# A two-layer hybrid trunk on one core: the high part of the modulated activations moves to ScalarE, the masked B to another pool, the zero states to DRAM

## The chip, the cores and the metric

One core of a Trainium2 chip runs the whole program in one launch. The metric is the device time of one execution in microseconds; the kernel before takes 3178.77 us (median of three runs).

## What is computed

The reference is a trunk of two layers over 1024 latent tokens and 256 context tokens of width 1024, in float32. Cut to what matters here:

```python
for l in range(DEPTH):
    u_ctx = modulate(rmsnorm(h_ctx, norm_mix_pre[l]), m_ctx[0], m_ctx[1])
    u_lat = modulate(rmsnorm(h_lat, norm_mix_pre[l]), m_lat[0], m_lat[1])
    a_ctx, a_lat = mixer_block(u_ctx, u_lat, ...)
    h_lat = h_lat + m_lat[2] * rmsnorm(a_lat, norm_mix_post[l])
    v_lat = modulate(rmsnorm(h_lat, norm_ffn_pre[l]), m_lat[3], m_lat[4])
    f_lat = conv_ffn(v_lat, ...)
    h_lat = h_lat + m_lat[5] * rmsnorm(f_lat, norm_ffn_post[l])
    ...
```

`mixer_block` projects u with one matrix into three groups of heads, a bidirectional Mamba-2 SSD, a neighbourhood attention and a bidirectional HGRN2, and joins their outputs in one output projection. In the second layer the context is not carried further. The SSD works in chunks of 128 tokens: for a chunk

```python
scores = jnp.einsum('btgn,bsgn->btsg', c_c, b_c)
y = jnp.einsum('btsg,btsgh,bsghp->btghp', scores, decay, x_c)
y = y + jnp.einsum('btgn,bghnp->btghp', c_c, h) * jnp.exp(cum)[..., None]
```

where h is the state that enters the chunk; it is zero for the first chunk of each direction.

## The kernel before

Tokens are cut into three blocks: block 0 is the context (two tiles of 128 tokens), blocks 1 and 2 hold four tiles of latent tokens each. Matrix products are made in three terms, since the fast operand type (fp32r) keeps only the leading bits of a float32: each activation and each weight is split into a high part H, rounded to fp32r, and a low part L, the float32 value less H; the products are H·wH, L·wH and H·wL.

**Modulated activations.** `xn_to_u` (L498) turns normalized token tiles into the transposed, modulated activations u. For each of eight tiles of 128 features TensorE transposes into a PSUM tile of tag "m"; ScalarE reads it, applies scale and shift and writes x into the SBUF tile S_xu (L168); `split(..., "p")` (L485) has GpSimd copy x, rounded, into U_uH (L490), and VectorE writes U_uL = x - H (L177). In some calls x is also stored to uD. The calls are made at the start, in the post that ends each mixer (layer 0 and layer 1), where u feeds the FFN, and in the post before layer 1: 136 feature tiles in all, of which 16, at the start, have 512 columns and 120 have 256. `post` (L539) runs around these calls: squares for the norm on ScalarE (the tile "junk", L168, with a short read of the accumulator), residual additions on GpSimd (L589), scaling of normalized tiles on GpSimd (L496) and ScalarE. "A unit" below is one call with two token tiles, eight feature tiles of 256 columns.

**The SSD outputs.** The scan over chunks leaves the entering states in a D tile, D_Us, and stores them to DRAM (hsD). Then `ssd_body` (L1365) goes through the chunks with a lag of three (SSD_LAG). For a chunk `ssd_load` (L1290) takes a D tile "sc" of five slices: slice 0 the two entering states, loaded from hsD or, for the first chunk of a direction, cleared by GpSimd (L1297); slice 1 the inputs (xtD); slices 2 and 3 hold ei, written by `ssd_weights`; half of slice 4 the two masked copies of B, made by GpSimd in `pmask` (L1287), one for each group g. `ssd_weights` (L1312) makes the weights of a group: S_R with D_sv and with the constant scr give exponents in "m" tiles (the matmuls S_R,D_sv and scr), ScalarE takes their exponential into S_E, GpSimd adds both directions (L1332), the matmul pg (L1330; F_cv,D_sc in the rows) multiplies the masked B by C, and VectorE multiplies. `ssd_outputs` then multiplies with states and inputs (S_E,D_sc and D_sc in the rows, L1342 on). The output projection's first half, `out_first` (L1458), is woven into this body as its filler (`weave`, L84): its products F_wo,U_m and w_wo,U_m stand between the SSD's own on TensorE. Its weights come through `load_wo` (L1429): four `wr` tiles for each half, loaded from DRAM and split into H and L. `mix_second` (L1410) takes `wr` tiles named gate.

**What sets the order.** All SBUF tiles come from one pool by tag, with a fixed number of buffers, and a tile waits until the buffer's last reader is done. All loads and stores are issued by SyncE (L163) in one queue. The order on each engine is fixed when the program is built, by the framework's timeline simulation (`schedule_with_timeline_sim=True`, L1930); on the chip every engine runs its own list in order and waits at its head. The numbers of buffers:

```python
BUFS = {"U": 10, "F": 10, "D": 3, "wr": 4, "w": 4, "S": 8, "E": 3, "O": 1}
PB = {"g": 2, "m": 6}
```

Of the kernel before, what the change touches and what calls it, by code (L numbers as in the profile page):

```python
# [8 lines left out]
F32 = mybir.dt.float32  # L9
# [4 lines left out]
AF = mybir.ActivationFunctionType  # L14
ALU = mybir.AluOpType
# [113 lines left out]
class Kern:  # L129
# [368 lines left out]
    def xn_to_u(self, b, xns, mod, u=None, o0=0, keep=None):  # L498

        n = 128 * len(xns)  # L500
        who = 1 if b == 0 else 0
        u = u or self.new_u(b)
        for ft in range(KT):
            pp = self.p("m")
            for i, xn in enumerate(xns):
                o = 128 * (ft % 4)
                self.tr(pp[:, 128 * i:128 * i + 128], xn[ft // 4][:, o:o + 128])
            x = self.t("S", [128, 512], name="xu")[:, 0:n]
            self.act(x, pp[:, 0:n], AF.Identity, scale=mod[:, who, 1, ft:ft + 1], bias=mod[:, who, 0, ft:ft + 1])
            self.split(u["H"][ft][:, o0:o0 + n], u["L"][ft][:, o0:o0 + n], x, "p")  # L510
            if keep is not None and b:
                self.dma(keep[ft, :, BLK[b][0] + o0:BLK[b][0] + o0 + n], x)
        return u
# [775 lines left out]

    def ssd_load(self, c, rows, cols, B):  # L1290
        tsl = slice(128 * c, 128 * c + 128)
        u = self.t("D", [128, 5, 512], name="sc")
        xz = self.t("F", [128, 2, 4, 128], name="xz")
        for d, i in ((0, c), (1, ORD_B.index(c))):
            hp = slice(64 * d, 64 * d + 64)
            if i == 0:
                self.nc.gpsimd.memset(u[hp, 0, :], 0.0)  # L1297
            else:
                self.dma(u[hp, 0, :], self.hsD[i, hp, :])
        self.dma(u[:, 1, :], self.xtD[tsl, :])  # L1300
        self.dma(xz[:, 0], self.xD[:, :, tsl].rearrange("j p t -> p j t"))
        self.dma(xz[:, 1], self.zD[:, :, tsl].rearrange("j p t -> p j t"))
        r = self.t("S", [128, 4, 128], F32R, name="R")
        self.pmask(r, rows[:, tsl].bitcast(F32), self.scs[:, 0:4], 4)
        o = 512 * (c % 2)
        cs = cols[:, 1, o:o + 512].rearrange("p (a b) -> p a b", b=128)
        self.pmask(cs, cols[:, 0, tsl].bitcast(F32), self.scs[:, 4:8], 4)
        o = 128 * c + (1 if c < 2 else 2)
        self.pmask(u[:, 4, 0:256].rearrange("p (a b) -> p a b", b=128), B[:, o:o + 128], self.scs[:, 8:10], 2)
        return u, xz, r, cs  # L1310

    def ssd_weights(self, Cm, c, g, u, r, cs):  # L1312

        o0 = 128 * c + (1 if c < 2 else 2)
        csl = slice(o0, o0 + 128)
        Es = []
        for d in range(2):
            ps = self.p("m")
            self.mm(ps, cs[:, 2 * g + d, :], r, stop=False)
            self.mm(ps, self.identr, self.late[d].unsqueeze(1).to_broadcast([128, 4, 128]), start=False)  # L1320
            e = self.t("S", [128, 4, 128], name="E")
            self.act(e.rearrange("p a b -> p (a b)"), ps, AF.Exp)
            Es.append(e)
        ps = self.p("m")
        self.mm(ps, self.sel[g], r)
        ei = u[:, 2 + g, :]
        self.act(ei, ps, AF.Exp)
        ei = ei.rearrange("p (h t) -> p h t", h=4)
        pg = self.p("m")
        self.mm(pg[:, 0:128], u[:, 4, 128 * g:128 * g + 128], Cm[g][:, csl])  # L1330
        w = Es[0]
        self.nc.gpsimd.tensor_tensor(out=w, in0=w, in1=Es[1], op=ALU.add)  # L1332
        self.nc.vector.tensor_tensor(out=ei, in0=ei, in1=Cm[g][:, csl].unsqueeze(1).to_broadcast([128, 4, 128]), op=ALU.mult)
        self.tt(w, w, pg[:, 0:128].unsqueeze(1).to_broadcast([128, 4, 128]), ALU.mult)
        return w, ei
# [461 lines left out]
    def run(self):  # L1797
        A = self.A
        self.adaD, self.adaP, self.adaN, self.ada_pend, self.ada_todo = {}, {}, {}, [], []
        self.consts()  # L1800
        self.cond()
        X, Wh = [], []
        mod = self.first_mod({2: lambda: X.append(self.first_norm(0)),
                              KT - 1: lambda: Wh.append(self.load_wt(0, *HEAD[0]))})
        Wh.append(self.load_wt(0, *HEAD[1]))
        self.more_consts()
        X.append(self.first_norm(1))
        U = {0: self.xn_to_u(0, X[0], mod)}
        X.append(self.first_norm(2))
        for b in (1, 2):  # L1810
            U[b] = self.xn_to_u(b, X[b], mod)
        C = {0: self.layer_cols(0)}
        self.lower_bounds()
        h1 = [self.dram([T, DM], f"h1_{l}") for l in range(2)]
        h2 = self.dram([T, DM], "h2")
        self.mixD = self.dram([8, 128, T], "mixD")
        self.zD = self.dram([4, 128, T], "zD")
        self.xD = self.dram([4, 128, T], "xD")
        self.accD = self.dram([T, DM], "accD")
        self.uD = self.dram([KT, 128, T], "uD")  # L1820
        self.hidD = [self.dram([NT, 128, len(grp), 128], f"hid{p}") for p, grp in enumerate(PASSES)]
        self.gD = self.dram([2, 128, T], "gD")
        self.iD = self.dram([T, 256], "iD")
        self.xtD = self.dram([T, 512], "xtD")
        self.vD = self.dram([T, 256], "vD")
        self.cvD = self.dram([2, 32, T], "cvD")
        self.hsD = self.dram([NT, 128, 512], "hsD")
        self.ada_todo = [(0, i, kt, q) for i in (1, 2) for q in range(4) for kt in range(KT)]
        for l in range(2):
            clo = 0 if l == 0 else 2  # L1830
            lat = [0, 1, 2] if l == 0 else [1, 2]
            U = self.layer(l, U, C, clo, lat, h1, h2, Wh)
# [102 lines left out]
```

## Time and profile before

| what | value |
|---|---|
| time, median of three runs | 3178.77 us (3176.94 to 3183.29) |
| time of the profiled execution | 3183.62 us |
| span of the profiled execution | 3181.8 us |
| mean clock granted to TensorE, of full speed | 0.973 |
| TensorE matmuls busy | 3013.4 us, 95% |
| VectorE busy | 1851.6 us, 58% |
| ScalarE busy | 1347.9 us, 42% |
| GpSimd busy | 769.8 us, 24% |

The profile is of one execution; its span begins with the first and ends with the last instruction, and the time is 1.8 us longer. Busy shares are means over stages that have different limits. In the rows PE is TensorE, PEld its weight loads, DVE is VectorE, ACT ScalarE, POOL GpSimd and SP SyncE; an entry in brackets at the end of a timeline row is the time the engine was idle before it and what ended that. Names are those of the program's tiles, tag first: U_uH is the high part of u.

### The profile page before, as it was taken

Reading aid. Unit: us, or ns where it says so; the run is one execution under the profiler, and the core shown is the slowest. Engines: PE = TensorE matmul, PEld = TensorE weight load, DVE = VectorE, ACT = ScalarE, POOL = GpSimd, SP = SyncE. Lnnn points to the kernel's source line nnn. Section 1 sums busy time; section 2 is a strip of 40 time slices with the busy share of each in tenths; the row PEclk is TensorE's granted clock in tenths of the full one; section 3 lists DMA queues with packets and bytes.
Section 4 is the critical chain, followed back from the end, with each engine's and each line's share of the span. In section 5 each row is a group of like instructions: output and inputs, shape, how many; then the busy total and the mean of one; then the engine's idle time right before and its main releaser. Section 6 shows DMA issues by size and latency. Waiting matters only on the chain. (4 is left out here: it accounts for less than half of the span.)

```text
span 3181.8 us, 55600 instructions
## 1 busy us (share of the span) xinstructions
PE 3013.4 (95%) x21478; PEld 2468.8 (78%) x21478; DVE 1851.6 (58%) x3443; ACT 1347.9 (42%) x2605; POOL 769.8 (24%) x847
## 2 busy tenths in 40 slices
PE   6999999979999999998999899999989899999998
PEld 4977877767778888886777797777767788887886
DVE  5253544568876665563344826554668876667346
ACT  4225625644543333343112633745545544445222
POOL 2000101146423333330000400101254344442002
PEclk8999999989999999999999999999999999999999
DMA  6224143366552222236465412221457532224242
GB/s 239 85 87 112 44 120 92 118 187 195 190 180 65 65 75 70 68 89 183 147 184 166 128 46 79 58 77 55 123 181 225 170 93 82 82 80 142 85 134 96
DMA packets 440649, 373.59 MB, mean 117 GB/s; under 512 B 28188, under 2 KB 360880, under 8 KB 439360
## 3 DMA queue, kind: packets, MB, share of 16 engines
q1 hardware_dynamic: 440384, 370.04, 38.4%
q8 instruction: 169, 2.77, 0.4%
q14 instruction: 96, 0.79, 0.1%
HBM read 265.17 MB, written 95.30 MB: 113 GB/s over the span
## 5 line engine op out<-in xcount | busy, mean ns | idle before, releaser
L189 PE MATMUL m_p<-U_dw,S_hH 128*128 128x512 f32 x1296 | 405.6, 392 | 1.2 <-ACT S_hH L171 1.2
L189 PE MATMUL g_p<-U_uH,w_wH 128*128 128x512 f32 (+1 forms) x1192 | 288.3, 375 | 26.3 <-POOL U_uH L490 13.5
L189 PE MATMUL m_p<-U_uH,w_wo 128*128 128x512 f32 x1120 | 306.5, 396 | 0.0
L189 PEld LDWEIGHTS m_p<-U_dw,S_hH 128*128 128x128 f32 x1296 | 243.6, 189 | 56.1 <-issue 3.8
L189 PE MATMUL g_p<-U_uL,w_wH 128*128 128x512 f32 (+1 forms) x1192 | 274.0, 367 | 0.0
L189 PE MATMUL g_p<-U_uH,w_wL 128*128 128x512 f32 (+1 forms) x1192 | 269.9, 362 | 2.0 <-issue 2.0
L189 PEld LDWEIGHTS g_p<-U_uH,w_wH 128*128 128x128 f32 x1192 | 206.5, 197 | 71.1 <-POOL U_uH L490 20.3
L189 PE MATMUL m_p<-U_dw,S_hL 128*128 128x512 f32 x648 | 254.2, 392 | 1.4 <-DVE S_hL L177 1.4
L189 PEld LDWEIGHTS m_p<-U_uH,w_wo 128*128 128x128 f32 x1120 | 207.9, 188 | 47.4 <-issue 0.2
L189 PEld LDWEIGHTS g_p<-U_uL,w_wH 128*128 128x128 f32 x1192 | 204.6, 198 | 34.3 <-issue 2.3
L189 PEld LDWEIGHTS g_p<-U_uH,w_wL 128*128 128x128 f32 x1192 | 199.9, 192 | 37.3 <-issue 4.2
L189 PE MATMUL m_p<-D_su,w_wo 128*128 128x512 f32 x800 | 206.2, 395 | 0.0
L177 DVE TENSOR_TENSOR w_wo<-wr_wr,w_wo 128x512 fp32r<-128x512 f32 x168 | 144.4, 860 | 102.4 <-ACT w_wo L171 101.7
L186 DVE SCALAR_TENSOR_TENSOR F_fc<-F_raw,colB,F_fc 128x1281 f32<-128x1281 f32 (+3 forms) x102 | 162.2, 1591 | 51.6 <-ACT F_fc L168 51.4
L177 DVE TENSOR_TENSOR S_hL<-S_hL,S_hH 128x512 fp32r<-128x512 f32 (+1 forms) x90 | 69.4, 771 | 189.6 <-ACT S_hH L171 189.4
L171 ACT CAST S_hH<-S_hL 128x512 fp32r<-128x512 f32 (+1 forms) x90 | 59.7, 663 | 278.7 <-DMA S_hL<-hid 254.9
L189 PEld LDWEIGHTS m_p<-D_su,w_wo 128*128 128x128 f32 x800 | 148.9, 188 | 34.1
L171 ACT CAST w_wo<-wr_wr 128x512 fp32r<-128x512 f32 x168 | 103.3, 619 | 160.3 <-PE m_p L189 101.1
L189 PE MATMUL m_p<-F_su,w_wo 128*128 128x512 f32 x640 | 161.7, 394 | 0.0
L1642 POOL TENSOR_TENSOR wr_t<-E_wr,E_wr 128x512 f32<-128x512 f32 x40 | 56.3, 1408 | 403.7 <-DMA E_wr<-in_ffn_w_up 335.5
L189 PE MATMUL m_p<-U_uL,w_wo 128*128 128x512 f32 x560 | 153.5, 395 | 0.0
L189 PEld LDWEIGHTS m_p<-U_dw,S_hL 128*128 128x128 f32 x648 | 122.0, 188 | 29.3 <-issue 2.2
(377 smaller groups left out, 6217.1 us busy)
## 6 DMA issues: line engine op xcount, KB each, us to landing
wr_aw<-in_ada_w SPq DMA_DIRECT2D x160, 256.0 KB
wr_wr<-in_ffn_w_up SPq DMA_DIRECT2D x96, 256.0 KB
wr_wr<-in_w_in SPq DMA_DIRECT2D x88, 256.0 KB
wr_wrd<-in_ffn_w_down SPq DMA_DIRECT2D x88, 256.0 KB
E_wr<-in_ffn_w_up SPq DMA_DIRECT2D x80, 256.0 KB
hid<-S_u SPq DMA_DIRECT2D x80, 256.0 KB
S_hL<-hid SPq DMA_DIRECT2D x54, 256.0 KB
h<-D_acc SPq DMA_DIRECT2D x45, 256.0 KB
```

What stands on the lines that cost most here:

```text
L171: self.nc.scalar.copy(out, in_)
L177: self.nc.vector.tensor_tensor(out=out, in0=a, in1=b, op=op)
L186: self.nc.vector.scalar_tensor_tensor(out=out, in0=a, scalar=s, in1=b, op0=op0, op1=op1)
L189: self.nc.tensor.matmul(out, lhsT=lhsT, rhs=rhs, start=start, stop=stop)
L1642: padd = lambda o, x, y, op=ALU.add: gp.tensor_tensor(out=o, in0=x, in1=y, op=op)
```

## The change

It has three parts. In `xn_to_u` ScalarE reads the PSUM tile twice, once into U_uH with rounding and once into S_xu; GpSimd's copy at L490 goes, VectorE's subtraction stays. The PSUM tile is held until the second read. In `ssd_load` the D tile has four slices, and the masked B goes to a tile mb of tag "wr", 128 x 256, held until the second group's pg matmul (a D buffer keeps its size, which other tiles of the tag set). The zero states are loaded like the others: a tile of zeros is written to hsD[0] at the start, and the two clears by GpSimd become two loads of 128 KB.

```diff
--- before.py
+++ after.py
@@ -506,8 +506,10 @@
                 o = 128 * (ft % 4)
                 self.tr(pp[:, 128 * i:128 * i + 128], xn[ft // 4][:, o:o + 128])
             x = self.t("S", [128, 512], name="xu")[:, 0:n]
-            self.act(x, pp[:, 0:n], AF.Identity, scale=mod[:, who, 1, ft:ft + 1], bias=mod[:, who, 0, ft:ft + 1])
-            self.split(u["H"][ft][:, o0:o0 + n], u["L"][ft][:, o0:o0 + n], x, "p")
+            h = u["H"][ft][:, o0:o0 + n]
+            for y in (h, x):
+                self.act(y, pp[:, 0:n], AF.Identity, scale=mod[:, who, 1, ft:ft + 1], bias=mod[:, who, 0, ft:ft + 1])
+            self.tt(u["L"][ft][:, o0:o0 + n], x, h.bitcast(F32), ALU.subtract)
             if keep is not None and b:
                 self.dma(keep[ft, :, BLK[b][0] + o0:BLK[b][0] + o0 + n], x)
         return u
@@ -1289,14 +1291,11 @@
 
     def ssd_load(self, c, rows, cols, B):
         tsl = slice(128 * c, 128 * c + 128)
-        u = self.t("D", [128, 5, 512], name="sc")
+        u = self.t("D", [128, 4, 512], name="sc")
         xz = self.t("F", [128, 2, 4, 128], name="xz")
         for d, i in ((0, c), (1, ORD_B.index(c))):
             hp = slice(64 * d, 64 * d + 64)
-            if i == 0:
-                self.nc.gpsimd.memset(u[hp, 0, :], 0.0)
-            else:
-                self.dma(u[hp, 0, :], self.hsD[i, hp, :])
+            self.dma(u[hp, 0, :], self.hsD[i, hp, :])
         self.dma(u[:, 1, :], self.xtD[tsl, :])
         self.dma(xz[:, 0], self.xD[:, :, tsl].rearrange("j p t -> p j t"))
         self.dma(xz[:, 1], self.zD[:, :, tsl].rearrange("j p t -> p j t"))
@@ -1306,10 +1305,11 @@
         cs = cols[:, 1, o:o + 512].rearrange("p (a b) -> p a b", b=128)
         self.pmask(cs, cols[:, 0, tsl].bitcast(F32), self.scs[:, 4:8], 4)
         o = 128 * c + (1 if c < 2 else 2)
-        self.pmask(u[:, 4, 0:256].rearrange("p (a b) -> p a b", b=128), B[:, o:o + 128], self.scs[:, 8:10], 2)
-        return u, xz, r, cs
-
-    def ssd_weights(self, Cm, c, g, u, r, cs):
+        mb = self.t("wr", [128, 256], name="mb")
+        self.pmask(mb.rearrange("p (a b) -> p a b", b=128), B[:, o:o + 128], self.scs[:, 8:10], 2)
+        return u, xz, r, cs, mb
+
+    def ssd_weights(self, Cm, c, g, u, r, cs, mb):
 
         o0 = 128 * c + (1 if c < 2 else 2)
         csl = slice(o0, o0 + 128)
@@ -1327,7 +1327,7 @@
         self.act(ei, ps, AF.Exp)
         ei = ei.rearrange("p (h t) -> p h t", h=4)
         pg = self.p("m")
-        self.mm(pg[:, 0:128], u[:, 4, 128 * g:128 * g + 128], Cm[g][:, csl])
+        self.mm(pg[:, 0:128], mb[:, 128 * g:128 * g + 128], Cm[g][:, csl])
         w = Es[0]
         self.nc.gpsimd.tensor_tensor(out=w, in0=w, in1=Es[1], op=ALU.add)
         self.nc.vector.tensor_tensor(out=ei, in0=ei, in1=Cm[g][:, csl].unsqueeze(1).to_broadcast([128, 4, 128]), op=ALU.mult)
@@ -1825,6 +1825,9 @@
         self.vD = self.dram([T, 256], "vD")
         self.cvD = self.dram([2, 32, T], "cvD")
         self.hsD = self.dram([NT, 128, 512], "hsD")
+        zero = self.t("S", [128, 512], name="zero")
+        self.nc.gpsimd.memset(zero, 0.0)
+        self.dma(self.hsD[0], zero)
         self.ada_todo = [(0, i, kt, q) for i in (1, 2) for q in range(4) for kt in range(KT)]
         for l in range(2):
             clo = 0 if l == 0 else 2
```

Line numbers after the change are larger by two or three (L1287 becomes L1289). The order on the engines moves with it. Three places are shown, before and after, each as one piece of the list of one engine.

GpSimd, layer 0, as the SSD outputs begin (D_sc is the chunk's tile, F_cv holds B, wr_gate belongs to `mix_second`, E_xw to the scan; S_R is the first chunk's mask of the row sums). Before:

```order
L1252 TENSOR_TENSOR E_xw_7266<-S_xT_7194,tdt_1581 128x512
L1297 MEMSET D_sc_7606 64x512
L1252 TENSOR_TENSOR E_xw_7281<-S_xT_7260,tdt_1581 128x512
L1287 TENSOR_TENSOR D_sc_7606<-F_cv_6033,scs_263 128x256
L1424 TENSOR_TENSOR wr_gate_7468<-U_m_7460,wr_gate_7468 128x512
L1424 TENSOR_TENSOR wr_gate_7474<-U_m_7460,wr_gate_7474 128x512
L1252 TENSOR_TENSOR E_xw_7449<-S_xT_7346,tdt_1581 128x256
L1252 TENSOR_TENSOR E_xw_7522<-S_xT_7429,tdt_1581 128x512
L1287 TENSOR_TENSOR S_R_7613<-F_sr_6590,scs_263 128x512
```

After:

```order
L1254 TENSOR_TENSOR E_xw_7269<-S_xT_7197,tdt_1584 128x512
L1289 TENSOR_TENSOR wr_mb_7619<-F_cv_6036,scs_263 128x256
L1254 TENSOR_TENSOR E_xw_7284<-S_xT_7263,tdt_1584 128x512
L1289 TENSOR_TENSOR wr_mb_7667<-F_cv_6036,scs_263 128x256
L1424 TENSOR_TENSOR wr_gate_7471<-U_m_7463,wr_gate_7471 128x512
L1424 TENSOR_TENSOR wr_gate_7477<-U_m_7463,wr_gate_7477 128x512
L1289 TENSOR_TENSOR wr_mb_7740<-F_cv_6036,scs_263 128x256
L1289 TENSOR_TENSOR wr_mb_7849<-F_cv_6036,scs_263 128x256
L1254 TENSOR_TENSOR E_xw_7452<-S_xT_7349,tdt_1584 128x256
L1254 TENSOR_TENSOR E_xw_7525<-S_xT_7432,tdt_1584 128x512
L1289 TENSOR_TENSOR S_R_7616<-F_sr_6593,scs_263 128x512
```

The clear is gone, and the masks of four chunks, in the four `wr` buffers, stand ahead of the first chunk's S_R; before, one mask did.

SyncE, the same place (wr_wr<-in_w_out are weights of `out_first`, second half; accD<-E_o stores its results; hsD<-D_Us stores the states). Before, the four weights are issued long ahead of the states' store:

```order
L164 DMA xtD_615<-S_xT_7260 128x4x128
L164 DMA wr_wr_7914<-in_w_out 128x512
L164 DMA wr_wr_7918<-in_w_out 128x512
L164 DMA accD_606<-E_o_7408 128x512
L164 DMA wr_wr_7924<-in_w_out 128x512
L164 DMA wr_wr_7928<-in_w_out 128x512
L164 DMA accD_606<-E_o_7432 128x512
```

After, they stand behind that store and between the loads of the chunks:

```order
L164 DMA hsD_618<-D_Us_7143 64x9x256 x2
L164 DMA wr_wr_7921<-in_w_out 128x512
L164 DMA accD_606<-E_o_7810 128x512
L164 DMA D_sc_7609<-hsD_618 64x512
L164 DMA D_sc_7657<-hsD_618 64x512 x2
L164 DMA D_sc_7657<-xtD_615 128x512
L164 DMA accD_606<-E_o_7869 128x512
L164 DMA wr_wr_7925<-in_w_out 128x512
L164 DMA wr_wr_7931<-in_w_out 128x512
L164 DMA D_sc_7730<-hsD_618 64x512 x2
L164 DMA D_sc_7730<-xtD_615 128x512
L164 DMA wr_wr_7935<-in_w_out 128x512
```

The first of the four is now directly behind the store of the states, the last behind the loads of the third chunk.

ScalarE, the start, the tiles of block 2 (E_vx and E_ix empty the "g" tiles of the head projections). Before:

```order
L168 ACTIVATE S_xu_476<-m_p_471,modc_215 128x512
L168 ACTIVATE S_xu_485<-m_p_480,modc_215 128x512
L168 ACTIVATE S_xu_494<-m_p_489,modc_215 128x512
L168 ACTIVATE S_xu_503<-m_p_498,modc_215 128x512
L168 ACTIVATE S_xu_512<-m_p_507,modc_215 128x512
L168 ACTIVATE S_xu_521<-m_p_516,modc_215 128x512
L171 COPY E_ix_759<-g_p_734 128x256
L168 ACTIVATE S_xu_530<-m_p_525,modc_215 128x512
L168 ACTIVATE S_xu_539<-m_p_534,modc_215 128x512
L171 COPY E_vx_788<-g_p_763 128x256
```

After:

```order
L168 ACTIVATE U_uH_468<-m_p_507,modc_215 128x512
L168 ACTIVATE S_xu_512<-m_p_507,modc_215 128x512
L171 COPY E_vx_734<-g_p_709 128x256
L168 ACTIVATE U_uH_468<-m_p_516,modc_215 128x512
L168 ACTIVATE S_xu_521<-m_p_516,modc_215 128x512
L168 ACTIVATE U_uH_468<-m_p_525,modc_215 128x512
L168 ACTIVATE S_xu_530<-m_p_525,modc_215 128x512
L168 ACTIVATE U_uH_468<-m_p_534,modc_215 128x512
L168 ACTIVATE S_xu_539<-m_p_534,modc_215 128x512
L171 COPY E_ix_762<-g_p_737 128x256
```

The copy E_ix stood between the sixth and the seventh x; now it stands behind the last of eight pairs. The squares of block 2's tiles (junk<-F_h) have moved from behind block 1's tiles to ahead of them.

## Rows read from the trace of the kernel before

**Rows 1.** the page, part 1: busy us (share) xinstructions of each engine

```profile
PE 3013.4 (95%) x21478; PEld 2468.8 (78%) x21478; DVE 1851.6 (58%) x3443; ACT 1347.9 (42%) x2605; POOL 769.8 (24%) x847
```

**Rows 2.** TensorE's waits <- what ended them: us, times, longest us

```profile
PE g_p L189 <- POOL U_uH L490: 13.5, 13, 2.3
...
PE m_p L189 <- POOL D_sc L1287: 13.1, 4, 7.2
```

**Rows 3.** the same for 800 to 960 us, then for 2430 to 2540 us

```profile
PE g_p L189 <- POOL U_uH L490: 6.7, 6, 2.3
...
PE g_p L189 <- POOL U_uH L490: 6.8, 7, 1.8
```

**Rows 4.** instructions on tile S_xu: xcount, ns min/median/max, first and last start

```profile
L168 ACT ACTIVATE S_xu<-m_p,modc x136: 544/565/825, 35.7 to 2506.5; 128x256 f32<-128x256 f32 x120, 128x512 f32<-128x512 f32 x16
...
L490 POOL TENSOR_SCALAR U_uH<-S_xu x136: 399/567/1157, 36.3 to 2507.3; 128x256 fp32r<-128x256 f32 x120, 128x512 fp32r<-128x512 f32 x16
```

**Rows 5.** timeline of ScalarE: start us, us, operation, xcount, [idle before <- releaser]

```profile
54.73 4.12 ACT L168 ACTIVATE S_xu<-m_p,modc 128x512 f32<-128x512 f32 x6 [0.46 <-PE m_p L194]
...
58.72 0.65 ACT L168 ACTIVATE junk<-F_h 128x512 bf16<-128x512 f32 x1
...
70.37 4.12 ACT L168 ACTIVATE S_xu<-m_p,modc 128x512 f32<-128x512 f32 x6 [4.13 <-PE m_p L194]
...
74.36 0.39 ACT L171 COPY E_ix<-g_p 128x256 f32<-128x256 f32 x1
...
890.38 2.39 ACT L168 ACTIVATE S_xu<-m_p,modc 128x256 f32<-128x256 f32 x5
```

**Rows 6.** timeline of GpSimd, layer 0's SSD stage and post

```profile
695.68 0.52 POOL L1297 MEMSET D_sc<- 64x512 f32 x1 [5.98 <-DMA hsD<-D_Us]
...
696.28 0.61 POOL L1287 TENSOR_TENSOR D_sc<-F_cv,scs 128x256 f32<-128x256 f32 x1
...
878.06 1.69 POOL L589 TENSOR_TENSOR F_accf<-F_accf,S_hres 128x512 f32<-128x512 f32 x1 [0.62 <-DVE F_accf L186]
```

**Rows 7.** timeline of TensorE: start, layer 0's SSD stage, layer 0's post

```profile
77.37 1.86 PE L189 MATMUL g_p<-F_wtH,U_uH 128*128 128x272 f32 x8 [2.03 <-DVE O_dtr L174]
...
696.95 0.80 PE L189 MATMUL m_p<-F_cv,D_sc 128*128 128x128 f32 x2 [4.20 <-POOL D_sc L1287]
...
700.23 0.70 PE L189 MATMUL m_p<-S_E,D_sc 128*64 128x128 f32 x4
...
712.04 0.35 PE L189 MATMUL m_p<-cf,F_xz 128*128 128x2 f32 x2 [3.85 <-POOL S_E L1332]
...
880.62 0.79 PE L189 MATMUL g_p<-U_uH,w_wH 128*128 128x256 f32 x2 [2.28 <-POOL U_uH L490]
...
891.65 3.91 PE L189 MATMUL g_p<-U_uH,w_wH 128*128 128x256 f32 x15
```

**Rows 8.** busy us (x) of PE, PEld, DVE, ACT, POOL; clock, DMA share, GB/s

```profile
837.00:895.00 58.00, 48.86 (x291) 42.52 (x289) 46.94 (x111) 41.59 (x98) 30.04 (x47) 0.85 0.50 168
1767.00:1840.00 73.00, 64.89 (x404) 58.05 (x405) 60.05 (x151) 49.19 (x120) 37.40 (x52) 0.93 0.40 124
2451.00:2508.00 57.00, 46.14 (x269) 39.87 (x268) 46.56 (x110) 39.59 (x93) 30.15 (x45) 0.91 0.57 186
```

**Rows 9.** timeline of TensorE, layer 1's SSD stage

```profile
2354.40 0.80 PE L189 MATMUL m_p<-F_cv,D_sc 128*128 128x128 f32 x2 [7.24 <-POOL D_sc L1287]
...
2357.69 0.51 PE L189 MATMUL m_p<-S_E,D_sc 128*64 128x128 f32 x4
```

**Rows 10.** windows as in rows 8, of 2350 to 2360 us

```profile
2350.00:2360.00 10.00, 5.60 (x43) 4.68 (x44) 5.46 (x6) 3.50 (x6) 5.28 (x5) 0.66 0.83 228
```

**Rows 11.** timeline of SyncE's DMA issues, SSD stages of layers 0 and 1

```profile
695.50 1.14 SPq L164 DMA_DIRECT2D D_sc<-hsD  x2
...
703.28 1.10 SPq L164 DMA_DIRECT2D D_sc<-hsD  x2
...
2352.14 3.23 SPq L164 DMA_DIRECT2D D_sc<-hsD  x4
```

## The prediction

> **What bounds the kernel now.** I read the page first, then the waits, then the posts by stretches, then single chains. TensorE is busy for 3013.4 of 3181.8 us [rows 1], so almost all of the time is its matmuls, and an edit that adds or removes no matmul is worth only what it does to the 168 us in which TensorE is idle or to the clock granted to it. The list of TensorE's own waits says which idle time the change aims at: 13.5 us in 13 waits for the high part U_uH that GpSimd writes at L490, and 13.1 us in 4 waits for L1287, the masked B in D_sc [rows 2]. The first lies in two stretches only, 6.7 us in layer 0's post and 6.8 us in layer 1's [rows 3]. The start (30 to 130 us) and the post before layer 1 (1760 to 1900 us) have no such wait of TensorE: the same GpSimd step runs there, but other work ends the waits. All 26.6 us are 0.84% of the span; about 0.2% (6.4 us) is what a measurement of this kernel can tell from no change.
>
> **The high part moves from GpSimd to ScalarE.** 136 GpSimd instructions of 567 ns (median) go, 77 us; 136 ScalarE instructions come, each a second read of the PSUM tile. The present read S_xu takes 565 ns alone [rows 4], and back to back five take 2.39 us and six of 512 columns 4.12 us [rows 5]: 0.48 and 0.69 us apiece. VectorE's subtract stays. So a unit of eight tiles of 256 columns costs ScalarE 8 x 0.48 = 3.8 us more, and the first high part of a unit comes one GpSimd step (0.57 us) sooner.
>
> *The two FFN posts and the post before layer 1.* What the hop costs today is seen at 880: GpSimd takes up an addition at L589, 1.69 us long [rows 6], between two high parts, and a second one behind the next, and TensorE stands 2.28 us before the next matmul [rows 7]. The waits of over 1 us of this kind are six, 10.5 us in the two posts. With GpSimd free of U_uH the additions no longer stand in front of it. But ScalarE must have room for its part. Of layer 0's post (837 to 895 us) ScalarE is busy 41.59 of 58 us; 40 tiles at 0.48 add 19.2, and 60.8 does not fit in 58. Before layer 1, 49.19 + 19.2 = 68.4 of 73 us; in layer 1's post, with 32 tiles, 39.59 + 15.4 = 55 of 57 [rows 8]. What ScalarE does there (squares for the next norm, casts, gate copies) is what the next unit waits for. In the last unit of a post nothing else is in front: today the eight x come 0.48 us apart and GpSimd keeps pace, TensorE's first 15 high matmuls take 3.91 us [rows 7]; afterwards the high parts come 0.96 us apart, since ScalarE writes high and x in turn, and the eighth is ready about 7 x 0.48 = 3.4 us later, less the 0.57 of the hop: 2.8 us, about 2.5 of which TensorE, which has only a few transposes to put in between, waits. I take: middle units, half of the 10.5 us come back (the other half turns into waits for ScalarE), -5; two last units +5; post before layer 1, where ScalarE is full and TensorE had nothing to gain, +1. Ends: -13.5 (all waits gone, nothing new) and +11.4 (nothing gained, three times a whole 3.8).
>
> The Trainium skill, page "ScalarE: Activation LUTs", section "Rules for kernel authors", advises VectorE rather than ScalarE for multiplications and additions, which speaks against a second affine pass on ScalarE. The trace does not bear its alternative out in these stretches: VectorE is the fuller engine in all three posts, 46.94 against 41.59 us in the first [rows 8]. By that rule the time would be the one of the second rival below.
>
> *The start.* Here both block-1 and block-2 tiles are 512 wide: 16 more ScalarE instructions of 0.69 us = 11 us between 54.73 and 76 [rows 5]. ScalarE has 4.13 us of idle before the second block [rows 5], and the new order runs the squares of block 2 before block 1's tiles, so that block 2 can follow directly; about 11 - 4 - 3 (four of those squares, 0.65 each and a short read [rows 5]) = 4 us are left by which the last x is late. The copy E_ix that empties one of two g tiles, now between the sixth and seventh tile, stands behind the last tile in the new order, and TensorE, which restarts at 77.37 and is full from there [rows 7], waits for it: +4, ends 0 (its wait of 2.03 hides it) and +6.
>
> **The masked B and the zero states.** Each layer's SSD outputs start with a D slot that comes free only when the states (D_Us) have been stored. In layer 0 GpSimd waits 5.98 us, clears half a tile (0.52), masks B (0.61) [rows 6]; TensorE stands 4.20 us, until 696.95 [rows 7]. In layer 1 it stands 7.24 us, until 2354.40 [rows 9], and its clock in 2350 to 2360 averages 0.66 [rows 10]. With mb in a wr tile that matmul and the S_R matmuls behind it no longer wait. But what follows needs the stored states themselves: the loads D_sc<-hsD are issued at 695.50 and at 2352.14, in four instructions of 3.23 us in layer 1 [rows 11], and the first output matmul S_E,D_sc runs at 700.23 and 2357.69 [rows 7, 9]. So the end of the wait moves from the mask to the load: of 4.20 us I take -2 (GpSimd's queue is free of one clear and two masks, 0.52 + 2 x 0.61 = 1.7 us, before the S_E that ends the 3.85 us wait at 712.04 [rows 7]); of layer 1's 7.24 I take -2, since a load issued at 2352.1 to 2355.4 needs still to land, and lets the outputs begin hardly before 2356. Ends: -5.2 and 0; -7.2 and 0. The two zero loads cost SyncE about 0.6 us each (two such issues took 1.14 [rows 11]); the clears were GpSimd's, so nothing waits for them now. The first 256 KB store of zeros and its clear lie under the opening loads: 0.
>
> Sum: -5 + 5 + 1 + 4 - 2 - 2 = +1 us on the profiled execution (3183.6, itself 4.85 above the median of 3178.77), so I put +1 on the median: **3180 us**. The ends add up to -25.9 and +17.4.
>
> **Rivals.** *Both waits come back (3160).* If ScalarE's idle time in the posts is mostly where the new reads fall, the 10.5 us return whole, the last units lose half of what I charged, and the mask's 13.1 us return to 8: -10.5 + 3 + 1 + 2 - 8 = -13, and about -6 more where TensorE, no longer stopped, keeps its clock (0.66 in 2350 to 2360 [rows 10] is 3 us lost in ten, in two places). For it: both waits are real and in order at the head of TensorE's queue. Against it: the full ScalarE and the state loads above.
>
> *ScalarE becomes the bound (3192).* In the posts it is asked for 184 of 188 us in sum (60.8 + 68.4 + 55), in order, behind transposes that wait for TensorE. If every pair pushes the squares of the next unit, each of the three posts loses a unit's 3.8 us and the start 6: 11.4 + 6 - 4 (SSD) = +13. It decides from the point at which ScalarE has no idle stretch left between 837 and 890. Against it: the x half may come late without harm to the high matmuls, and GpSimd's additions come sooner.
>
> *The wr ring binds (3187).* The four wr tiles hold mixer weights too. In the new order four masks are made early and hold all four; the out projection's weights, on SyncE before the state loads so far, are issued between and behind them. If TensorE waits for the last of them, it does so until a load issued behind the third chunk's (703.28 plus 1.10 [rows 11]) has landed and been cast, some 4 us behind its place, in each layer: +8. The same ring is how the change could fail to do what it says: a mask that waits for a weight slot instead of a D slot.
>
> **Chances.** My forecast, near balance, 0.37; both waits back 0.33; ScalarE the bound 0.21; wr ring 0.09. Faster by over 0.2% is the first rival, 0.33; slower by as much the other two, 0.30. The forecast's own range is 3173 to 3185. The range given, 3158 to 3192, takes in all four values and leaves out about a fifth: a gain beyond 21 us, a loss beyond 13.
>
> **What would show it.** Right: waits for U_uH by TensorE are named ScalarE and sum to 6 to 10 us; ScalarE busy near 1417 us (1347.9 + 120 x 0.48 + 16 x 0.69) and GpSimd near 690; the L1287 wait gone and one of 5 us or so for D_sc<-hsD or D_sc in layer 1; last high part of the last unit some 2.5 us later after the transposes. Wrong: posts shorter by over 5 us each (first rival); waits for S_R or for weights w_wo, F_wo at the SSD stages (third); TensorE's restart at 77 us unmoved.

## The result and the profile after

The changed kernel takes 3214.15 us (median of four runs, 3210.44 to 3221.48) beside 3181.03 us for the kernel before on the same chip: ratio 1.0109, 95% interval 1.009 to 1.0128, **about 35 us slower** (33 by the two medians). The prediction was 3180 us with a range to 3192. Differences below are such ratios, less one, times some 3180 us unless a profile is named; numbers in square brackets behind a ratio are its 95% interval. A profile is of one execution.

The page of the kernel after, part 1:

```profile
PE 3035.5 (94%) x21478; PEld 2478.7 (77%) x21478; DVE 1838.4 (57%) x3443; ACT 1409.2 (44%) x2739; POOL 689.8 (21%) x710
```

ScalarE and GpSimd moved as forecast (1417 and 690 were expected; [rows 1]). The surprise stands at the front: the same 21478 matmuls are busy for 22.1 us longer. The profiled execution (3221.48 us, span 3219.7, mean granted clock 0.965) has a span 37.9 us longer than before; 22.1 of that is longer busy time of TensorE and only 15.8 is TensorE standing still.

TensorE's waits in the kernel after (what they ended on: us, times, longest us):

```profile
PE m_p L189 <- DMA wr_aw<-in_ada_w: 27.0, 17, 4.5
...
PE g_p L189 <- ACT U_uH L168: 10.6, 21, 0.7
PE g_p L189 <- ACT F_wo L171: 9.9, 2, 6.1
PE m_p L194 <- ACT S_xu L168: 8.4, 7, 2.3
...
PE g_p L189 <- ACT F_raw L171: 4.3, 2, 3.3
...
PE m_p L194 <- POOL D_acc L496: 3.2, 2, 3.0
```

Both waits that the change aimed at have left the list [rows 2]. The one for U_uH has become 21 waits for ScalarE's U_uH, together somewhat shorter (10.6 for 13.5 us) and in smaller pieces; in place of that for the masked B (13.1 us) stand two for F_wo. Longer than before are the waits of transposes for a PSUM tile still being read (S_xu, 3.7 us in three before) and, largest, those of matmuls for wr_aw, weights of the conditioning (adaLN) that the change does not mention: 18.9 us in 18 waits before. The wait for GpSimd's scaling (D_acc, L496) is new.

To place the loss, the same five stretches of TensorE's work are cut out of both traces at the same instructions: the HGRN2 scans with the projections woven in, SSD and post of layer 0, the post before layer 1, SSD and post of layer 1. The kernel before (columns as in [rows 8]; the count behind PE's busy time shows that the work is the same, up to a few records):

```profile
384.00:511.00 127.00, 117.30 (x1982) 94.21 (x1982) 55.20 (x100) 48.65 (x93) 1.41 (x9) 0.93 0.44 120
511.00:818.00 307.00, 281.39 (x1840) 226.92 (x1839) 204.95 (x456) 161.88 (x345) 117.18 (x119) 0.97 0.51 156
818.00:940.00 122.00, 109.65 (x638) 92.49 (x637) 95.64 (x196) 68.69 (x151) 47.84 (x67) 0.92 0.55 178
1728.00:1869.00 141.00, 130.11 (x801) 115.61 (x800) 89.31 (x220) 69.60 (x169) 45.38 (x57) 0.96 0.30 95
...
2335.00:2535.00 200.00, 175.71 (x1049) 145.15 (x1046) 159.03 (x324) 108.36 (x227) 103.72 (x101) 0.96 0.61 192
```

The same of the kernel after:

```profile
382.90:524.50 141.60, 123.89 (x1982) 98.40 (x1982) 54.52 (x100) 48.51 (x93) 1.39 (x9) 0.87 0.39 108
524.50:837.20 312.70, 286.28 (x1840) 229.90 (x1839) 210.74 (x456) 161.43 (x345) 118.98 (x117) 0.95 0.50 154
837.20:961.50 124.30, 110.66 (x636) 91.01 (x635) 90.19 (x196) 86.03 (x191) 25.59 (x27) 0.92 0.54 175
1746.90:1890.50 143.60, 132.19 (x801) 117.01 (x800) 84.17 (x221) 87.70 (x211) 23.71 (x17) 0.94 0.28 93
...
2354.60:2573.70 219.10, 188.38 (x1049) 152.94 (x1046) 161.82 (x332) 126.25 (x265) 84.06 (x67) 0.91 0.57 181
```

The stretches grew by 14.6, 5.7, 2.3, 2.6 and 19.1 us; the start added 4.1, the stretches between gave 10.5 back, in sum 37.9. Two things are to be seen. The first row holds nothing that was edited, and loses 14.6. And in the two stretches that lose most the clock fell as well (0.93 to 0.87, 0.96 to 0.91): of 14.6 us 8.0 is more idle time and 6.6 longer busy time, of 19.1 us 6.4 and 12.7. A single place of TensorE's timeline in the kernel after shows what that is:

```profile
2502.45 0.44 PE L194 MATMUL m_p<-cf,D_acc 128*128 128x128 f32 x2 [2.29 <-ACT S_xu L168]
...
2511.51 1.91 PE L189 MATMUL g_p<-U_uH,w_wL 128*128 128x256 f32 x8
...
2543.98 1.07 PE L189 MATMUL g_p<-U_uH,w_wL 128*128 128x256 f32 x8
```

From 2511.5 to 2515 the granted clock is 0.50 (1.2 GHz), and eight matmuls U_uH,w_wL take 1.91 us; at 2543.98, at 1.00 (2.4 GHz), eight such take 1.07. The clock is still 1.00 from 2495 to the end of the wait of 2.29 us for S_xu, averages 0.56 from 2502.45 to 2505 and is 0.50 from there to 2515. Three more waits, of 1.12, 0.64 and 0.72 us for S_xu and U_uH, end later, at 2504.00, 2505.34 and 2506.86.

### The profile page after: what moved, and what is told of

It reads as the page before. It is cut to its first block, busy times and chain, and to the rows that moved or that the text cites. A ratio compares the mean times of both kernels' runs of the same rounds, so it can differ in the third digit from the quotient of the medians.

```text
span 3219.7 us, 55524 instructions
## 1 busy us (share of the span) xinstructions
PE 3035.5 (94%) x21478; PEld 2478.7 (77%) x21478; DVE 1838.4 (57%) x3443; ACT 1409.2 (44%) x2739; POOL 689.8 (21%) x710
## 5 line engine op out<-in xcount | busy, mean ns | idle before, releaser
L189 PEld LDWEIGHTS m_p<-F_su,w_wo 128*128 128x128 f32 x640 | 120.2, 188 | 28.6
```

Source lines behind the costliest of these rows:

```text
L189: self.nc.tensor.matmul(out, lhsT=lhsT, rhs=rhs, start=start, stop=stop)
```

## The experiments

Each kernel ran in five rounds beside the kernel before on the same chip. Where one does the high part by ScalarE only in some calls, its edit is this, with the condition `both` given at the run (arguments cut at "..."):

```diff
-            self.act(x, pp[:, 0:n], AF.Identity, scale=..., bias=...)
-            self.split(u["H"][ft][:, o0:o0 + n], u["L"][ft][:, o0:o0 + n], x, "p")
+            h = u["H"][ft][:, o0:o0 + n]
+            for y in ((h, x) if both else (x,)):
+                self.act(y, pp[:, 0:n], AF.Identity, scale=..., bias=...)
+            if not both:
+                self.nc.gpsimd.tensor_scalar(out=h, in0=x, scalar1=1.0, scalar2=0.0, op0=ALU.mult, op1=ALU.add)
+            self.tt(u["L"][ft][:, o0:o0 + n], x, h.bitcast(F32), ALU.subtract)
```

### The two halves of the change

**e1_high_only**: the edit of `xn_to_u` alone (`both` always true).

> The first part alone: high part and x both by ScalarE, mask and zero states as before. The whole change cost 33 us. Read between fixed places of TensorE's list in the two profiles, the start lost about 3 us, layer 0's post 8 and layer 1's post 8. If ScalarE is the main cause (theory A), this kernel is slower than before by 20 to 33 us. If the wr ring and ScalarE share the loss (theory R), by 12 to 19. If ScalarE costs nothing, within 5 of before. GpSimd's waits at L490 are gone from TensorE's list in any case.

Measured: 3204.01 beside 3178.22 us, 1.0075 [1.0058, 1.0092], +24 us. ScalarE is busy 1409.3 us; TensorE waits 11.7 us in 19 waits for U_uH by ScalarE, and 5.5 us for F_raw.

**e2_ssd_only**: the edits of `ssd_load`, `ssd_weights` and hsD[0], the high part left to GpSimd.

> Mask in a wr tile and zero states from DRAM together, high part by GpSimd as before. If the parts add up: 33 - 24 = 9 us slower than before (2 of the mask, 7 of the zero states). If they only cost in the company of the high part, within 4 of before.

Measured: 3184.56 beside 3179.73 us, 1.0017 [1.0008, 1.0026], +5 us. The wait for L1287 is gone, and 10.1 us in three waits for F_wo stand in its place. So the high part alone costs 24 us, and the SSD's edits, forecast at -4, cost 5; the 6 that are left are within what the intervals allow.

### The SSD's edits one by one

**e3_mask_only**: the masked B in a wr tile, the memsets kept. Here and in e6 and e15 the diff is cut: the mask and the matmul pg are pointed at mb as in the change, and the D tile has four slices.

```diff
-        u = self.t("D", [128, 5, 512], name="sc")
+        u = self.t("D", [128, 4, 512], name="sc")
+        mb = self.t("wr", [128, 256], name="mb")
```

> The mask alone: mb in a wr tile, GpSimd's clears and its high part as before. Theory R: the weights of the out projection are late, TensorE shows a wait for F_wo of some 6 us in layer 1's SSD stage and the kernel is 8 to 16 us slower than before. Theory A: within 5 us of before, or up to 8 faster, since the waits for L1287 (13.1 us) go.

Measured: 1.0006 [0.9994, 1.0019]: no difference that can be told. F_wo is waited for 12.7 us in three waits, where L1287 was 13.1 in four [rows 2].

**e4_zero_only**: the zero states loaded from hsD[0] in place of the memsets (the three lines that store the zeros are as in the change).

```diff
-            if i == 0:
-                self.nc.gpsimd.memset(u[hp, 0, :], 0.0)
-            else:
-                self.dma(u[hp, 0, :], self.hsD[i, hp, :])
+            self.dma(u[hp, 0, :], self.hsD[i, hp, :])
```

> The zero states alone: loaded from DRAM, mask in the D tile, high part by GpSimd. Every theory: within 4 us of before; the clear of 0.52 us and two issues of about 0.6 us on SyncE change places. A loss of more would put the loads of states behind each other on SyncE among the causes.

Measured: 1.0021 [1.001, 1.0032], +7 us, with the mask's wait still there (12.5 us in three) and 7.9 us in four for F_xz (DVE; 2.8 in three before). The loads of zeros were costed at nothing but SyncE's time; that they are not free is measured, why they cost 7 us is not shown. The profile cannot show it: its execution, 3183.13 us, is the fastest of the twelve and as long as that of the profile before.

**e6_mask_f_only**: the masked B in 256 more columns of the chunk's own F tile.

```diff
+        fx = self.t("F", [128, 1280], name="xz")
+        xz = fx[:, 0:1024].rearrange("p (a j t) -> p a j t", a=2, j=4)
+        mb = fx[:, 1024:1280]
```

> The mask in the last 256 columns of the chunk's F tile (F_xz, whose buffer has room), so that it leaves the D tile and takes no wr buffer; all else as before. Theory R: the weights are issued where they were, no wait for F_wo, and the time is 2 to 8 us below before (part of the 13.1 us of waits comes back). If leaving the D tile is itself the loss (the work behind the mask waits elsewhere), it is as slow as the mask in wr.

Measured: 1.0091 [1.0069, 1.0113], +29 us, the worst place of all, where 2 to 8 us of gain were expected. The F_wo wait is gone as expected, but TensorE waits 15.4 us in eight for F_xz and 6.9 in two for ScalarE's D_sc. What makes this place so dear stays open.

**e15_mask_e**: the masked B in an E tile (three buffers); all else as before.

```diff
+        mb = self.t("E", [128, 256], name="mb")
```

> The mask in a tile of tag E (three buffers, used by the scan before and by results of the out projection), clears and high part as before. The weights of the out projection are issued where they were. If the ring was what ate the gain of the mask in wr (12.7 us of waits for F_wo in place of 13.1 for L1287): 4 to 10 us faster than before. If the states and the D slot behind the mask are what counts, within 4 of before; if the F tile's result (28 slower) came from leaving the D tile at all, 15 or more slower.

Measured: 3174.61 beside 3179.73 us, 0.9983 [0.9972, 0.9993], **-5 us: faster than both kernels**. Neither the masked B nor F_wo is among its large waits any more. But the E buffers hold the results of the output projection too, and TensorE's waits for them have grown from 4.7 us:

```profile
PE g_p L189 <- ACT E_o L171: 11.2, 7, 3.8
```

The growth is in layer 0, where a new wait of 3.60 us at 699.9 stands close to the place of the 4.20 us for the mask [rows 7]. TensorE's timeline of this kernel in layer 1:

```profile
2342.63 0.38 PE L189 MATMUL m_p<-F_cv,E_mb 128*128 128x128 f32 x2
2342.95 0.44 PE L189 MATMUL m_p<-S_E,D_sc 128*64 128x128 f32 x4
2345.83 0.44 PE L189 MATMUL m_p<-D_sc 128*64 128x128 f32 x4 [2.44 <-DMA D_sc<-hsD]
```

In layer 1 the mask's matmul no longer waits for the mask, and the next thing that is late is the load of the states: 2.44 us in place of 7.24 [rows 9], just where the prediction put the end of the wait. The same idea in a wr tile ends elsewhere. TensorE in the kernel after, the same place:

```profile
2369.02 0.70 PE L189 MATMUL m_p<-S_E,D_sc 128*64 128x128 f32 x4
2375.86 4.18 PE L189 MATMUL g_p<-F_wo,U_m 128*128 128x512 f32 x9 [6.14 <-ACT F_wo L171]
```

ScalarE, the same kernel, layer 0 and layer 1:

```profile
713.49 0.62 ACT L171 CAST F_wo<-wr_wr 128x512 fp32r<-128x512 f32 x1 [4.50 <-DMA wr_wr<-in_w_out]
...
2374.05 1.09 ACT L168 ACTIVATE D_sc<-m_p 128x512 f32<-128x512 f32 x2 [5.18 <-DMA hsD<-D_Us]
2375.19 0.62 ACT L171 CAST F_wo<-wr_wr 128x512 fp32r<-128x512 f32 x1
```

The masks hold wr buffers, so the weights of the output projection are loaded late and their casts stand late in ScalarE's order. In layer 0 the cast waits for the weight itself (4.50 us). In layer 1 it stands behind the exponentials ei, which are still written into the chunk's D tile and so wait 5.18 us for the store of the states: the old D slot, reached by another way. ScalarE in e15, layer 1, has the casts ahead of that wait, as has the kernel before (casts at 2338.45, the exponential behind a wait of 6.09 us at 2353.68):

```profile
2329.11 1.14 ACT L171 CAST F_wo<-wr_wr 128x512 fp32r<-128x512 f32 x2
...
2341.90 0.60 ACT L168 ACTIVATE D_sc<-m_p 128x512 f32<-128x512 f32 x1 [4.07 <-DMA hsD<-D_Us]
```

### The high part: load, lateness, places

**e7_dummy**: the kernel before with a second ScalarE read of each PSUM tile into a junk tile that nobody reads; GpSimd still makes the high part.

```diff
+            self.act(self.junk[:, 0:n], pp[:, 0:n], AF.Identity, scale=..., bias=...)
```

> The kernel before, with a second read of each of the 136 PSUM tiles by ScalarE into the scratch tile junk; GpSimd still writes the high part from x. This adds ScalarE's load without moving the high part. Theory L (ScalarE's room in the posts is what the change costs): 18 to 30 us slower than before, like the high part alone (+24), with ScalarE busy near 1409 us. Theory H (the loss comes from where the high parts and x now stand: x comes every 0.96 us, the last of a unit late): at most 10 us slower.

Measured: 3224.24 beside 3177.02 us, 1.0153 [1.0133, 1.0172], +49 us. Its TensorE waits:

```profile
PE m_p L194 <- ACT junk L168: 25.8, 8, 10.1
...
PE g_p L189 <- POOL U_uH L490: 17.7, 15, 7.9
```

136 more reads on ScalarE, with no other edit, cost twice what the real edit does (49 against 24), more than either expectation. The transposes wait for the second read, which keeps the PSUM tile from coming free. That is not the shape of the real edit's loss, though. Part 1 of the two pages, e7 and then e1:

```profile
PE 3016.4 (94%) x21478; PEld 2468.7 (77%) x21478; DVE 1840.6 (57%) x3443; ACT 1417.5 (44%) x2739; POOL 766.6 (24%) x847
PE 3028.2 (95%) x21478; PEld 2477.4 (77%) x21478; DVE 1834.4 (57%) x3443; ACT 1409.3 (44%) x2739; POOL 692.2 (22%) x711
```

The span of e7 (3214.9 us) is 33.1 us longer than before, of which 3.0 is busy time of TensorE; that of e1 (3203.2 us) 21.4 longer, of which 14.8 is busy time. So e7 shows that second reads can cost as much as was lost; that ScalarE's load is what costs in the real edit it does not show.

**e10_half**: `both = ft % 2 == 0`, every second feature tile.

> ScalarE writes the high part of the even feature tiles, GpSimd that of the odd ones. If ScalarE's full queue is the cause (theory L), half the load costs less than half of the 24 us, since ScalarE has idle time up to a point: 0 to 10 us slower. If each high part that ScalarE makes costs the same, 12. If both engines side by side make the posts shorter, faster than before by up to 6.

Measured: 1.0075 [1.0062, 1.0087], +24 us: half the added reads cost as much as all of them (e1). The expectation of a loss in proportion to ScalarE's load (12 us or less) fell here: the size does not follow the sum of ScalarE's time. That it follows from which instruction is late in which order is the reading of the runs below; this run alone does not show it.

**e8_ffn_posts**: `both = keep is not None`, the two FFN posts alone.

> High part by ScalarE only in the two posts that feed the FFN (72 tiles of 136). In the profile of the high part alone the post of layer 0 lost some 3 us against before, that of layer 1 some 13, so 12 to 18 us slower than before. If the start and the post before layer 1 carry the loss instead, under 6.

Measured: 1.0054 [1.0041, 1.0067], +17 us. In its profile, 11.1 us longer than before, TensorE stands still as long as before (168.5 against 168.4 us) and is busy 11.0 us longer.

**e16_x_first**: e8 with x read ahead of h in each pair.

```diff
-            for y in ((h, x) if both else (x,)):
+            for y in ((x, h) if both else (x,)):
```

> The high part by ScalarE in the two posts that feed the FFN, as in the run that was 17 us slower than before, but of each pair x is written first and the high part second. If the high matmuls' lateness carries the loss: 18 to 22 slower than before, since every high part is 0.48 us later. If x's lateness does (store to uD, reload, casts ahead of F_raw): 12 to 16.

Measured: 1.0065 [1.0052, 1.0078], +21 us. The interval meets that of e8, so no effect of the order within the pair can be told; an earlier x, which was expected to bring the time below e8 if it decided, does not cure the loss. The wait for F_raw treated under the next run is as long as in e8 (3.34 and 3.38 us).

**e14_last_pool**: e8 without the last unit, `both = keep is not None and not (b == 2 and o0 == 256)`.

> High part by ScalarE in the two posts that feed the FFN, except in their last unit, where GpSimd makes it. Against the run with all units (17 us slower than before): if the last unit carries the loss (pairs 0.96 us apart, x stored late to uD, and behind it casts of reloaded x that stand ahead of the copy F_raw), 7 to 9 us come back, 8 to 10 slower than before. If the middle units carry it (squares of the next unit pushed back), 14 to 17 slower still.

Measured: 1.0015 [1.0002, 1.0028], +5 us, less than either expectation. So about 12 of the 17 us come from the last unit of the two posts (by difference; the intervals are 13 to 21 and 1 to 9), the other three or four units of each cost 5 together. ScalarE in the kernel after, end of layer 1's last unit:

```profile
2541.24 0.64 ACT L168 ACTIVATE U_uH<-m_p,modc 128x256 fp32r<-128x256 f32 x1
2541.69 0.65 ACT L168 ACTIVATE S_xu<-m_p,modc 128x256 f32<-128x256 f32 x1
2546.30 0.62 ACT L171 CAST D_su<-S_xs 128x512 fp32r<-128x512 f32 x1 [3.96 <-DVE S_xs L177]
...
2548.91 0.37 ACT L171 COPY F_raw<-g_p 128x256 f32<-128x256 f32 x1
```

TensorE, the same kernel and place:

```profile
2534.22 2.39 PE L194 MATMUL m_p<-cf,D_acc 128*128 128x128 f32 x10 [2.98 <-POOL D_acc L496]
...
2549.33 2.77 PE L189 MATMUL g_p<-U_uH,w_wH 128*128 128x512 f32 x8 [3.26 <-ACT F_raw L171]
```

The pairs last until 2542.3; x goes out to uD and comes back as S_xs, and its casts D_su wait for it. In the order after, the casts stand ahead of the copy F_raw that empties a g tile. So F_raw, whose matmuls end at about 2545, waits behind them, and TensorE behind F_raw for 3.26 us (5.06 in e1). ScalarE in the kernel before has F_raw ahead of the first cast:

```profile
2511.19 0.36 ACT L171 COPY F_raw<-g_p 128x256 f32<-128x256 f32 x1
2514.31 0.62 ACT L171 CAST D_su<-S_xs 128x512 fp32r<-128x512 f32 x1 [2.76 <-DVE S_xs L177]
```

ScalarE in e14, whose last unit is as before:

```profile
2505.85 3.85 ACT L168 ACTIVATE S_xu<-m_p,modc 128x256 f32<-128x256 f32 x8 [0.85 <-PE m_p L194]
...
2514.54 0.37 ACT L171 COPY F_raw<-g_p 128x256 f32<-128x256 f32 x1
...
2515.84 0.62 ACT L171 CAST D_su<-S_xs 128x512 fp32r<-128x512 f32 x1
```

Here eight reads take 3.85 us, F_raw stands ahead of the casts again, and TensorE's wait for F_raw in layer 1 is gone (one of 1.58 us in layer 0 is left; e8 has 1.43 there); the wait of 3.0 us for L496 stays. So the chain behind x is worth some 3 us of waiting out of the 12. Where the other 9 come from is not shown; e8's profile has its loss in TensorE's busy time.

### The start and the post before layer 1

**e9_start_mid**: `both = keep is None`, the start and the post before layer 1.

> The rest: high part by ScalarE only at the start and in the post before layer 1 (24 and 40 tiles). The profile of the high part alone shows the start 4.7 us late at 100 us (of which 1.5 is left at 350, where the loads set the pace) and the post before layer 1 2.5 us: 3 to 9 us slower. With the run before, the two should add up to 24.

Measured: 1.0064 [1.0051, 1.0078], +20 us, where 3 to 9 were expected.

**e11_start_only**: the start alone (`both = u is None` at the call).

> High part by ScalarE at the start alone (24 tiles). Theory S (the new order at the start shifts the order that is fixed at build time up to the HGRN2 stage, whose matmuls then wait for adaLN weights wr_aw at 390 to 505 us): 12 to 20 us slower than before, of which 4 to 6 stand at 120 us and some 10 more come between 390 and 505 us. If the start costs only what it loses there, 4 to 6.

Measured: 1.0036 [1.0023, 1.0048], +11 us, close to the 12 to 20 of the shifted order. What the edit does at its place is seen in the kernel after: the copies E_ix and E_vx stand behind the last pair of reads (82.61 and 82.86), and TensorE waits for one of them:

```profile
83.53 1.27 PE L189 MATMUL g_p<-F_wtH,U_uH 128*128 128x272 f32 x8 [1.07 <-ACT E_vx L171]
```

**e12_mid_only**: the post before layer 1 alone.

> High part by ScalarE in the post before layer 1 alone (40 tiles). The run with start and this post together lost some 4 us between 1730 and 1870 us: 2 to 6 us slower than before. With the start alone it should add up to the 20 of both.

Measured: 1.0015 [1.0003, 1.0027], +5 us.

**e13_no_start**: the whole change, but at the start the high part by GpSimd.

> The whole change, but GpSimd makes the high part at the start as before; masks, zero states and the posts as changed. Theory S: the order up to 600 us is that of before, and of the 33 us of the whole change 12 to 18 are gone: 15 to 21 us slower than before. If the start's share is only its own 4 to 6 us, 27 to 29.

Measured: 3203.01 beside 3179.75 us, 1.007 [1.0054, 1.0086], +22 us: without the start 12 of the 35 us come back, as e11 would have it. Most of the start's loss lies 300 us behind it. TensorE's waits for wr_aw from 385 to 530 us, in the kernels before, after, e11 and e13:

```profile
PE m_p L189 <- DMA wr_aw<-in_ada_w: 1.5, 3, 0.9
PE m_p L189 <- DMA wr_aw<-in_ada_w: 11.3, 5, 3.6
PE m_p L189 <- DMA wr_aw<-in_ada_w: 8.8, 5, 2.6
PE m_p L189 <- DMA wr_aw<-in_ada_w: 0.6, 1, 0.6
```

The order of TensorE's instructions and of SyncE's loads in the unedited HGRN2 stage differs in the kernels with the edited start (one order in e1, e9, e11 and after), and is that of before in e8 and e13. Two successive wr_aw groups in the kernel before:

```profile
425.14 0.62 PE L189 MATMUL m_p<-wr_aw,scol 128*2 128x128 f32 x16
...
425.94 2.13 PE L189 MATMUL g_p<-U_uH,w_wH 128*128 128x512 f32 x8
427.92 2.03 PE L189 MATMUL g_p<-U_uL,w_wH 128*128 128x512 f32 x8
429.78 2.03 PE L189 MATMUL g_p<-U_uH,w_wL 128*128 128x512 f32 x8
...
432.85 0.62 PE L189 MATMUL m_p<-wr_aw,scol 128*2 128x128 f32 x16
```

and in e11:

```profile
430.32 0.62 PE L189 MATMUL m_p<-wr_aw,scol 128*2 128x128 f32 x16 [1.15 <-DMA wr_aw<-in_ada_w]
430.87 1.90 PE L189 MATMUL g_p<-U_uH,w_wH 128*128 128x512 f32 x7
432.61 0.63 PE L189 MATMUL g_p<-U_uL,w_wH 128*128 128x512 f32 x2
...
435.62 0.62 PE L189 MATMUL m_p<-wr_aw,scol 128*2 128x128 f32 x16 [1.79 <-DMA wr_aw<-in_ada_w]
```

Between the two groups lay 28 matmuls of 512 columns (24 of them in these rows), now nine and some short ones. SyncE issued the last loads ahead of the second group at 425.61, 7.2 us before it, and the group did not wait; in e11 at 430.78, and the group begins 4.8 us later after a wait of 1.79 us. The matmuls were put where their data had not landed yet.

## Why the prediction was wrong, point by point

- **Both aimed waits.** Right that TensorE's waits for GpSimd's U_uH and for L1287 would go, that ScalarE would be busy near 1417 us, and that the high part's waits would return under ScalarE's name (6 to 10 us forecast, 10.6 measured). The wait for D_sc<-hsD or D_sc in layer 1, put among the signs of being right, did not come; that for F_wo, among the signs of the third rival, did.
- **Masked B, -2 in each layer.** Right in mechanism for layer 1, wrong in the place of the tile: with an E tile the wait there becomes the 2.44 us load of the states and the edit is worth -5 us (e15, [0.9972, 0.9993]), though waits for E_o take back part of it in layer 0; in a wr tile the ring (the four buffers that the tag's tiles take in turn) takes it back (e3, no difference). The wr rival, held at 0.09, is what happened in this part: waits for F_wo of 3.8 us in layer 0 and 6.1 in layer 1, where it was given 4 in each. In layer 0 by its own mechanism; in layer 1 through ScalarE's order and the D slot, which it did not see. The step "the two zero loads ... nothing waits for them" failed: +7 (e4). The terms -2 and -2 together measured +5 (e2).
- **The posts, -5 for middle units and +5 for last ones.** This is the term that failed most: 0 forecast, +17 measured (e8). The middle units gave back nothing (e14: +5). The last units cost about 12. The lateness of the high parts was foreseen: in layer 1's last unit the last one ends 7.7 us after the transposes begin, where it was 5.3. The chain behind x was not (uD, S_xs, D_su, and F_raw behind D_su in ScalarE's order, 3.4 us in e8). In sum the waits came out as priced: in e8's profile TensorE's idle time is that of before, and the loss is 11.0 us more busy time, which the term put at nothing.
- **The post before layer 1, +1.** Measured +5 [1, 9] (e12).
- **The start, +4.** The size was right at its place: TensorE is 4.1 us late at 121 us (the kernels with the start unedited pass there at 118.5 to 122.3 us, those with the whole start edited at 124.0 to 126.9). The mechanism was so only in part, and the agreement is partly luck: the copies do stand behind the last pair, but TensorE's wait there is 1.07 us, and of the 4.1 half is longer busy time (78.14 us before, 80.28 after, from 30 us on). And the term should have been 11 (e11): the remainder falls in the HGRN2 stage, which the forecast left untouched. The shifted order there is in the program as built, and could have been read before the run; only the edited places were compared.
- **The clock.** The sum priced waits by their length. In the profile 22.1 of the 37.9 us is more busy time of the same matmuls, with the granted clock lower (0.965 for 0.973). Only the first rival counted it, and there as a gain; its 3 us in ten is too much by its own row, where TensorE is busy 5.60 of the 10 us and a clock of 0.66 costs 1.9. The high part's waits shrank in sum from 13.5 to 10.6 us while their number grew from 13 to 21, but that more and shorter stops lower the clock is not shown: at the one place looked at it fell behind a stop of 2.29 us, and the shorter stops came later. What lowered the clock over the whole program stays open.
- **The second rival** (ScalarE becomes the bound, 3192) had the right sign and engine and missed the size. Its mechanism, a loss that grows with ScalarE's load, is not what e10 shows, where half the reads cost as much as all. It left out the order behind the posts, the clock, and the HGRN2 stage.

The parts do not add: e8, e11 and e12 make 33 us, e8 and e9 37, and e1, which is all of these, 24. Each edit gives a new order for the whole program. In the HGRN2 stage alone the kernels with the edited start lose between 4 and 15 us in their profiles (e10 4.1, e1 5.5, e11 7.5, e9 11.4, after 14.6). The order there does not set this alone: e1, e9, e11 and after have the same one. Nor is a single profile sharp: the kernels that have the order of before take 123.8 to 127.2 us in this stage, and the kernel before is the longest of them. What else sets it is open, as is e4's +7 and e6's +29.

## What to carry to other kernels

Where the order is fixed at build time, compare the whole order before and after, not the edited lines alone: an edit of the first 80 us moved instructions 300 us later and cost more there than at its place. Before a tile goes to another pool, list what else takes that pool's buffers and when: the same mask was worth +29, 0 or -5 us by its place alone. And moving work from one half-idle engine to another is safe only where the receiving engine has slack in the stage that counts: look at the last unit of a pipelined stage, at what comes behind its last instruction in the engine's order, and at TensorE's clock as well as at its waits: in e8's profile the loss was all busy time.

## What was not expected of the hardware

A loss need not show as waiting: in layer 1's SSD and post 6.4 us more idle time went with 12.7 us more busy time for 1049 matmuls, the granted clock falling from 0.96 to 0.91. A second ScalarE read of the same PSUM tile comes 0.45 us behind the first in a run of pairs (2541.24 and 2541.69), nearly the 0.48 us that was assumed; the price per instruction was right, and the loss came from elsewhere.
